# Letting each operation run where it ends first, with ScalarE as a third place for scaling probabilities

## The chip, the cores and the metric

The kernel runs on one core of a Trainium2 chip. The metric is the device time of one execution in microseconds (us); lower is better. Times are given as the median of several executions. The engines are named as the profile names them: PE is TensorE's matrix multiplication and PEld its weight load, DVE is VectorE, ACT is ScalarE, POOL is GpSimd, SP is SyncE.

## The reference

Two small transformer blocks run one after the other on one sequence of 512 tokens with 1024 features, all in float32. The first block has a layer of sparse attention (three gated branches: compressed, selected and windowed keys), a layer of windowed attention with a learned sink, and after each a feed-forward block with a short convolution. The second has a layer that mixes windowed attention with pooling over windows, a layer that mixes latent attention with a gated linear recurrence, and a squared-relu feed-forward block after each.

```python
def one_block(qb):                       # first layer, a block of 128 queries
    p_c = softmax(where(valid, sc, NEG)) * valid
    p_s = softmax(ss); p_w = softmax(where(m_w, sw, NEG))
    ...
    return gg[..., 0:1] * o_c + gg[..., 1:2] * o_s + gg[..., 2:3] * o_w
...
def conv_ffn(h, w_in, conv_w, conv_b, w_out):
    u = h @ w_in
    c = conv_b + conv_w[0] * up[:, 0:s] + ...   # three taps
    a, gate_in = split(c, 2)
    return (silu(a) * gate_in) @ w_out
...
def sq_relu_mlp(h, w1, w2):
    u = relu(h @ w1)
    return (u * u) @ w2
```

## The kernel before

Activations lie with features on the partitions and the 512 tokens along the free dimension. A float32 product is made of three products of rounded numbers: each operand is split into a high and a low part (`split` for activations, `load` for weights), and TensorE multiplies high by high, high by low and low by high (`mm3`). Every weight unit (128 x 1024) is fetched by a DMA into one of four `raw` buffers, copied to its high part, and the low part is the difference of the two (`copy` and `sub` in `load`); high and low lie in one of three `W` buffers.

The program is not written in the order in which it runs. Each helper call is recorded as an operation with an engine, its inputs and outputs, and, for some, alternatives on other engines (`alt`). A planner (`Recorder.order`) then plays the engines forward in time, with prices from `price` (cost: how long the engine is held; lat: when the result is there; lock: which other engine's use of SBUF it has to wait for). An engine that is free walks through its list of ready operations, ordered by rank (the recorded number, 1500 lower for weights), and takes the first that fits a buffer. The planned order is what is emitted; the chip then runs each engine's instructions in that order, with waits where data are needed. All instructions have one line in the profile, L698, the one that emits them.

Where an operation has an alternative, its first engine takes it whenever it comes to it. Another engine takes it when the work listed for the first engine (up to 12 ready operations, wherever they stand in the list, also those that can't start yet for want of a buffer) reaches a threshold:

```python
if op.eng != e:
    queue = sum(o.cost for _, _, o in ready[op.eng][:12] if not o.done)
    if queue + max(0, free_at[op.eng] - now) < SPILL[op.eng, e]:
        continue
```

Copies (`copy`) belong to ACT, with DVE as the other engine from 2.0 us; subtractions (`sub`, `tt(..., spare)`) belong to DVE, with POOL from 1.5 us; the scaling of a row of probabilities (`norm`) belongs to POOL, with DVE from 1.5 us; products by `ptt` are POOL's alone, and `tt` without `spare` is DVE's alone.

The stages follow one another: sparse attention (called nsa), feed-forward with convolution, windowed attention (swa), the same feed-forward again, pooling with attention (even), feed-forward (mlp), recurrence with latent attention (odd), mlp. In an attention stage the order of heads, query blocks and products is written out by hand in `ORDERS`. For a head, `scores` multiplies queries by keys, takes the maximum (DVE), the exponential with its sum (ACT), the reciprocal (DVE) and scales (`norm`); `product` transposes the probabilities on TensorE, splits them and multiplies by the values. In nsa, `norm` multiplies by the reciprocal and by the gate in one instruction with two scalars per row. ACT loads a table before a function that the loaded one doesn't hold; the planner holds such an operation back for up to `PATIENCE` (3 us) if its list still has others that need no load.

Of the kernel before, what the change touches and what calls it, by code (L numbers as in the profile page):

```python
# [11 lines left out]
AF = mybir.ActivationFunctionType  # L12
OP = mybir.AluOpType
AX = mybir.AxisListType

P = 128
S = 512
D = 1024
# [319 lines left out]
def _width(v):  # L338
# [13 lines left out]
SPILL = {("vector", "gpsimd"): 1.5, ("gpsimd", "vector"): 1.5, ("scalar", "vector"): 2.0, ("scalar", "gpsimd"): 2.0,  # L352
         ("vector", "scalar"): 1.0}
BOOST = 0
DMAQ = 2.0
HORIZON = 3000
ORDERS = {
# [28 lines left out]
PATIENCE = 3.0  # L386
# [4 lines left out]
class Recorder:  # L391
# [115 lines left out]
    def order(self):  # L507
# [4 lines left out]
        free_at = dict.fromkeys(engines, 0.0)  # L512
# [14 lines left out]
        front = 0  # L527
# [9 lines left out]
                heapq.heappush(wait[e], (op.ready, op.n, op))  # L537


        def oldest(kind):  # L540
            w = waiting[kind]
            while first[kind] < len(w) and w[first[kind]] in given:
                first[kind] += 1
            return w[first[kind]] if first[kind] < len(w) else -1
# [49 lines left out]
        while left:  # L594
# [7 lines left out]
            for e in engines:  # L602
# [6 lines left out]
                i = -1  # L609
                while i < min(len(ready[e]) - 1, 200):  # L610
                    i += 1
                    op = ready[e][i][2]
                    if op.done:
                        del ready[e][i]
                        i -= 1
                        continue
                    if op.eng != e:
                        queue = sum(o.cost for _, _, o in ready[op.eng][:12] if not o.done)
                        if queue + max(0, free_at[op.eng] - now) < SPILL[op.eng, e]:
                            continue  # L620
                    if e == "scalar" and op.table and table not in op.table and now - op.ready < PATIENCE:
                        if now - switched < PATIENCE or any(not o.table or table in o.table for _, _, o in ready[e][i + 1:]):
                            heapq.heappush(events, max(switched, op.ready) + PATIENCE + 1e-6)
                            continue
                    if e == "sync" and dma_free - now > DMAQ:
# [87 lines left out]
def F(ap):  # L713
    return ap.bitcast(F32)


def _body(tc, ctx, d, out):
# [74 lines left out]
    def tt(o, a, b, op, spare=False):  # L792
        kw = dict(out=o, in0=a, in1=b, op=op)
        nc.vector.tensor_tensor(**kw, alt=[["gpsimd", "tensor_tensor", (), kw]] if spare else None)

    def norm(o, i, a, b):
        nc.gpsimd.tensor_scalar(o, i, a, b, op0=OP.mult, op1=OP.mult, alt=[
            ["vector", "tensor_scalar", (o, i, a, b), {"op0": OP.mult, "op1": OP.mult}]])

    def ptt(o, a, b, op):  # L800
        nc.gpsimd.tensor_tensor(out=o, in0=a, in1=b, op=op)

    def sub(o, a, b):
        tt(o, a, b, OP.subtract, True)
# [168 lines left out]
    def rope(ps, cs, half):  # L973
        x, o = get(), get()
        copy(x, ps)
        if half == 32:
            for r in range(0, P, 32):
                nc.sync.dma_start(o[r:r + 32], x[r ^ 32:(r ^ 32) + 32])
            sw = o
        else:  # L980
            sw = get()
            nc.vector.stream_shuffle(sw, x, [n ^ 16 for n in range(32)])
        y = get()
        ptt(y, x, cs[0], OP.mult)
        tt(o, sw, cs[1], OP.mult)
        tt(o, o, y, OP.add, True)
        return o

# [72 lines left out]
    def nsa(x, epi, prepare, half):  # L1061
# [189 lines left out]
        def scores(g, qb, ty, h0):  # L1251
# [18 lines left out]
            for i in range(nh):  # L1270
                ei = F(e)[:, i * wd:(i + 1) * wd]
                act(ei, pv[:, i], AF.Exp, bias=nm[:, i:i + 1], accum_out=sm[:, i:i + 1])
            nc.vector.reciprocal(sm[:, 0:nh], sm[:, 0:nh])
            for i, (r, t) in enumerate(who):
                ei = F(e)[:, i * wd:(i + 1) * wd]
                gi = 3 * (4 * g + r) + t
                norm(ei, ei, sm[:, i:i + 1], gates[:, qb, gi:gi + 1])
                heads[g, qb, t, r] = ei

        def product(g, qb, ty, kb):  # L1280
# [23 lines left out]
    def sink_attn(qs, ks, vs, group, per, window, mask, sink, outs):  # L1304
# [5 lines left out]
        def scores(g, qb, h0):  # L1310
# [28 lines left out]
            nc.vector.reciprocal(sm[:, 0:per], sm[:, 0:per])  # L1339
            for i in range(per):  # L1340
                ei = ev[:, i, base:base + wd]
                norm(ei, ei, sm[:, i:i + 1], 1.0)
                heads[g, qb, h0 + i] = ei
            if over:
                nc.gpsimd.memset(ev[:, :, sc], 0.0)
# [175 lines left out]
    def odd(x, rb, half):  # L1521
# [185 lines left out]
        def scores(n, qb):  # L1707
# [7 lines left out]
            nc.vector.tensor_reduce(out=nm[:, 0:1], in_=ps, axis=AX.X, op=OP.max, negate=True)  # L1715
            act(F(e), ps, AF.Exp, bias=nm[:, 0:1], accum_out=sm[:, 0:1])
            nc.vector.reciprocal(sm[:, 0:1], sm[:, 0:1])
            norm(F(e), F(e), sm[:, 0:1], 1.0)
            es[n, qb] = e

        sums = {}
# [141 lines left out]
```

## Time and profile before

| | us |
|---|---|
| median of 3 executions | 2403.03 (2398.35 to 2403.59) |
| the profiled execution | 2399.78 |
| its span, first to last instruction | 2397.9 |
| TensorE busy in the span | 2280.3 (95%) |
| DVE busy | 1760.9 (73%) |
| POOL busy | 1254.6 (52%) |
| ACT busy | 701.8 (29%) |
| mean granted clock of TensorE | 0.976 of full speed |

The busy times are those of one execution. The share of an engine over the whole span is a mean over stages that differ much, so the rows below are taken by stage. In them a group of instructions is named by line, engine, operation and tiles (out<-in); S and D are tiles of 512 and 1024 columns in SBUF, `raw` and `W` the weight buffers, `bank` is PSUM, `small` holds 16 columns, `par` and `cst` are parameters and constants.

### The profile page before, as it was taken

What the parts mean: (1) busy time and instruction counts of PE and PEld (TensorE: products, weight loads), DVE (VectorE), ACT (ScalarE), POOL (GpSimd) and SP (SyncE); (2) the same over time, 40 slices, a digit from 0 to 9 for tenths busy, and PEclk for the clock granted to TensorE, in tenths of its full rate; (3) what the DMA queues carried; (4) which work ended last, traced back from release to release, by engine and by line L of the source; (5) the groups of instructions that cost most, each with busy time, mean ns of one, the idle gap of its engine ahead of it and who ended that gap; (6) DMA issues with size and microseconds to landing.
All of it is one profiled execution on the core that took longest, in us unless ns stands there. A gap on an engine that the chain in (4) does not pass through costs nothing.

```text
span 2397.9 us, 28536 instructions
## 1 busy us (share of the span) xinstructions
PE 2280.3 (95%) x10565; PEld 1857.6 (77%) x10565; DVE 1760.9 (73%) x2429; ACT 701.8 (29%) x1353; POOL 1254.6 (52%) x865
## 2 busy tenths in 40 slices
PE   9878999999999799999999799999999789999998
PEld 7766678888888578888888578888887568888888
DVE  7978888949499999949499897345358899643546
ACT  4435653202023463202014342000014584100003
POOL 5755636444447855444437745444466565444445
PEclk9979999999999899999999899999999989999999
DMA  6421102232225212332225213332243201222224
GB/s 208 137 75 49 54 23 88 97 106 97 97 84 185 87 36 85 101 106 97 97 82 182 71 52 99 102 109 97 97 154 115 66 27 62 97 97 97 97 97 132
DMA packets 77243, 230.02 MB, mean 96 GB/s; under 512 B 10288, under 2 KB 12976, under 8 KB 77104
## 3 DMA queue, kind: packets, MB, share of 16 engines
q1 hardware_dynamic: 75584, 226.89, 29.1%
q8 instruction: 83, 1.36, 0.2%
q10 hardware_dynamic: 1520, 1.32, 0.2%
q14 instruction: 56, 0.46, 0.1%
HBM read 206.67 MB, written 8.39 MB: 90 GB/s over the span
## 4 chain that ended last, share of the span: by engine, by line
PE 56%; DVE 6%; ACT 2%; issue 1%; POOL 1%; SPq 0%; DMA 0%; DVEq 0%; ACTq 0%; POOLq 0%
PE bank L698 56%; DVE S L698 4%; DVE small L698 1%; ACT S L698 1%; DVE D L698 1%; POOL S L698 0%; DVE W L698 0%; ACT W L698 0%; ACT L698 0%; POOL W L698 0%; ACT D L698 0%; SPq L698 0%; DVE bank L698 0%; DMA S<-S 0%; DVEq L1850 0%
## 5 line engine op out<-in xcount | busy, mean ns | idle before, releaser
L698 PE MATMUL bank<-S,W 128*128 128x512 f32 (+1 forms) x7972 | 1809.3, 387 | 9.9 <-POOL W L698 5.9
L698 PEld LDWEIGHTS bank<-S,W 128*128 128x128 f32 x7972 | 1472.6, 189 | 313.3 <-DVE S L698 7.8
L698 POOL TENSOR_TENSOR W<-raw,W 128x1024 fp32r<-128x1024 f32 (+2 forms) x288 | 693.3, 2408 | 708.3 <-DVE W L698 541.8
L698 DVE CAST W<-raw 128x1024 fp32r<-128x1024 f32 (+2 forms) x246 | 179.8, 731 | 460.5 <-issue 319.3
L698 POOL TENSOR_TENSOR S<-S,S 128x512 f32<-128x512 f32 (+3 forms) x203 | 327.4, 1618 | 234.7 <-DVE S L698 157.7
L698 ACT ACTIVATE S<-S 128x512 f32<-128x512 f32 (+2 forms) x220 | 137.4, 627 | 969.6 <-DVE S L698 951.9
L698 DVE TENSOR_TENSOR S<-bank,S 128x512 f32<-128x512 f32 (+5 forms) x429 | 264.5, 632 | 14.5 <-ACT S L698 7.0
L698 DVE SCALAR_TENSOR_TENSOR S<-S,par,S 128x511 f32<-128x511 f32 (+3 forms) x236 | 250.2, 1069 | 7.7 <-ACT S L698 2.6
L698 ACT ACTIVATE W<-raw 128x1024 fp32r<-128x1024 f32 (+2 forms) x132 | 133.7, 1015 | 298.2 <-PE bank L698 242.8
L698 DVE TENSOR_TENSOR S<-S,S 128x512 fp32r<-128x512 f32 (+3 forms) x210 | 193.4, 926 | 16.8 <-ACT S L698 4.7
L698 PE MATMUL bank<-S,D 128*128 128x512 f32 (+3 forms) x387 | 138.4, 431 | 26.1 <-DVE S L698 13.5
L698 DVE CAST S<-S 128x512 fp32r<-128x512 f32 (+1 forms) x126 | 120.2, 954 | 48.7 <-ACT S L698 44.0
L698 ACT ACTIVATE S<-bank,small 128x256 f32<-128x256 f32 (+6 forms) x245 | 127.5, 530 | 83.3 <-DVE small L698 74.8
L698 ACT ACTIVATE S<-bank 128x512 fp32r<-128x512 f32 (+5 forms) x179 | 102.8, 588 | 137.9 <-PE bank L698 116.1
L698 PE MATMUL bank<-D,W 128*128 128x512 f32 x536 | 139.8, 397 | 0.6 <-DVE W L698 0.6
L698 DVE TENSOR_TENSOR W<-raw,W 128x1024 fp32r<-128x1024 f32 (+2 forms) x90 | 124.7, 1385 | 13.6 <-ACT W L698 13.0
L698 PE MATMUL bank<-cst,S 128*128 128x128 f32 x710 | 115.5, 283 | 13.6 <-DVE S L698 7.9
L698 DVE TENSOR_REDUCE small<-bank 128x1 f32<-128x512 f32 (+7 forms) x201 | 119.9, 614 | 6.8 <-PE bank L698 5.2
L698 PEld LDWEIGHTS bank<-D,W 128*128 128x128 f32 x536 | 99.1, 188 | 20.4 <-ACT S L698 0.8
L698 PEld LDWEIGHTS bank<-cst,S 128*128 128x128 f32 x710 | 88.0, 145 | 33.8 <-DVE S L698 8.3
L698 DVE TENSOR_SCALAR S<-S,par 128x512 f32<-128x512 f32 (+1 forms) x62 | 112.3, 1812 | 2.1
L698 PEld LDWEIGHTS bank<-S,D 128*128 128x128 f32 x387 | 70.4, 197 | 51.4 <-DVE S L698 24.9
(122 smaller groups left out, 1398.3 us busy)
## 6 DMA issues: line engine op xcount, KB each, us to landing
raw<-in_f_in_dram SPq DMA_DIRECT2D x88, 512.0 KB, 3.2
raw<-in_m_out_dram SPq DMA_DIRECT2D x72, 512.0 KB, 3.2
raw<-in_m_in_dram SPq DMA_DIRECT2D x64, 512.0 KB, 3.3
raw<-in_f_out_dram SPq DMA_DIRECT2D x32, 512.0 KB, 3.2
raw<-in_a_in_dram SPq DMA_DIRECT2D x17, 512.0 KB, 3.5
raw<-in_o_in_dram SPq DMA_DIRECT2D x15, 512.0 KB, 3.4
S<-S SPq DMA_DIRECT2D x116, 64.0 KB, 2.0
raw<-in_f_out_dram SPq DMA_DIRECT2D x16, 384.0 KB, 2.9
```

Of the source, the lines that this page charges most:

```text
L698: r = getattr(getattr(nc, op.eng), name)(*args, **kw)
```

## The change

Four things change in the planner and its helpers. First, whether an engine takes an operation that has alternatives is decided by a comparison (`best`): for every engine that could do it, the planner adds the time until that engine is free and the costs of the operations of its own that stand ahead in its list (of the first 12), or the time until the other engine's hold on SBUF ends, to the operation's lat and to a tax of once its cost on POOL and DVE (none on ACT). An engine that isn't the one with the earliest end leaves the operation alone. Second, `norm` has one scalar per row and may run on ACT too; the gate of the nsa stage is multiplied into the reciprocals ahead of it, in a small product on DVE for each call of `scores`. Third, `ptt` may run on DVE and the second product of `rope` on POOL. Fourth, when the planner asks whether an ACT operation that needs a table load should be held back, operations beyond its horizon of 3000 recorded operations no longer count as others that need none.

```diff
--- before.py
+++ after.py
@@ -352,6 +352,9 @@
 SPILL = {("vector", "gpsimd"): 1.5, ("gpsimd", "vector"): 1.5, ("scalar", "vector"): 2.0, ("scalar", "gpsimd"): 2.0,
          ("vector", "scalar"): 1.0}
 BOOST = 0
+TAX = {"gpsimd": 1.0, "vector": 1.0}
+MARGIN = {}
+DEEP = 12
 DMAQ = 2.0
 HORIZON = 3000
 ORDERS = {
@@ -537,6 +540,29 @@
                 heapq.heappush(wait[e], (op.ready, op.n, op))
 
 
+        def cost_on(op, e):
+            return (op.cost, op.lat, op.lock) if e == op.eng else op.alt[e][1]
+
+        def best(op, e):
+
+            def wait(x):
+                lock = cost_on(op, x)[2]
+                return max(0.0, held["P"] - now) if lock == "D" else max(0.0, held["D"] - now) if lock else 0.0
+            here = wait(e) + cost_on(op, e)[1] + TAX.get(e, 0.0) * cost_on(op, e)[0]
+            for x in (op.eng, *op.alt):
+                if x == e:
+                    continue
+                q = max(0.0, free_at[x] - now)
+                for _, _, o in ready[x][:DEEP]:
+                    if o is op:
+                        break
+                    if not o.done and o.eng == x:
+                        q += o.cost
+                there = max(q, wait(x)) + cost_on(op, x)[1] + TAX.get(x, 0.0) * cost_on(op, x)[0]
+                if there + MARGIN.get((x, e), 0.0) < here:
+                    return False
+            return True
+
         def oldest(kind):
             w = waiting[kind]
             while first[kind] < len(w) and w[first[kind]] in given:
@@ -614,12 +640,12 @@
                         del ready[e][i]
                         i -= 1
                         continue
-                    if op.eng != e:
-                        queue = sum(o.cost for _, _, o in ready[op.eng][:12] if not o.done)
-                        if queue + max(0, free_at[op.eng] - now) < SPILL[op.eng, e]:
-                            continue
+                    if op.alt and not best(op, e):
+                        continue
                     if e == "scalar" and op.table and table not in op.table and now - op.ready < PATIENCE:
-                        if now - switched < PATIENCE or any(not o.table or table in o.table for _, _, o in ready[e][i + 1:]):
+                        if now - switched < PATIENCE or any(
+                                (not o.table or table in o.table) and o.n <= front + HORIZON
+                                for _, _, o in ready[e][i + 1:]):
                             heapq.heappush(events, max(switched, op.ready) + PATIENCE + 1e-6)
                             continue
                     if e == "sync" and dma_free - now > DMAQ:
@@ -793,12 +819,14 @@
         kw = dict(out=o, in0=a, in1=b, op=op)
         nc.vector.tensor_tensor(**kw, alt=[["gpsimd", "tensor_tensor", (), kw]] if spare else None)
 
-    def norm(o, i, a, b):
-        nc.gpsimd.tensor_scalar(o, i, a, b, op0=OP.mult, op1=OP.mult, alt=[
-            ["vector", "tensor_scalar", (o, i, a, b), {"op0": OP.mult, "op1": OP.mult}]])
+    def norm(o, i, a):
+        nc.gpsimd.tensor_scalar(o, i, a, None, op0=OP.mult, alt=[
+            ["vector", "tensor_scalar", (o, i, a, None), {"op0": OP.mult}],
+            ["scalar", "activation", (o, i, AF.Copy), {"scale": a}]])
 
     def ptt(o, a, b, op):
-        nc.gpsimd.tensor_tensor(out=o, in0=a, in1=b, op=op)
+        kw = dict(out=o, in0=a, in1=b, op=op)
+        nc.gpsimd.tensor_tensor(**kw, alt=[["vector", "tensor_tensor", (), kw]])
 
     def sub(o, a, b):
         tt(o, a, b, OP.subtract, True)
@@ -982,7 +1010,7 @@
             nc.vector.stream_shuffle(sw, x, [n ^ 16 for n in range(32)])
         y = get()
         ptt(y, x, cs[0], OP.mult)
-        tt(o, sw, cs[1], OP.mult)
+        tt(o, sw, cs[1], OP.mult, True)
         tt(o, o, y, OP.add, True)
         return o
 
@@ -1271,10 +1299,16 @@
                 ei = F(e)[:, i * wd:(i + 1) * wd]
                 act(ei, pv[:, i], AF.Exp, bias=nm[:, i:i + 1], accum_out=sm[:, i:i + 1])
             nc.vector.reciprocal(sm[:, 0:nh], sm[:, 0:nh])
+            gi = 3 * (4 * g + who[0][0]) + who[0][1]
+            if qb == 0:
+                gv = gates[:, qb, gi - 1:gi + 5].rearrange("p (r t) -> p r t", t=3)[:, :, 1:3]
+                sv = sm[:, 0:nh].rearrange("p (r t) -> p r t", t=2)
+            else:
+                gv, sv = gates[:, qb, gi:gi + 3 * nh - 2:3], sm[:, 0:nh]
+            tt(sv, sv, gv, OP.mult)
             for i, (r, t) in enumerate(who):
                 ei = F(e)[:, i * wd:(i + 1) * wd]
-                gi = 3 * (4 * g + r) + t
-                norm(ei, ei, sm[:, i:i + 1], gates[:, qb, gi:gi + 1])
+                norm(ei, ei, sm[:, i:i + 1])
                 heads[g, qb, t, r] = ei
 
         def product(g, qb, ty, kb):
@@ -1339,7 +1373,7 @@
             nc.vector.reciprocal(sm[:, 0:per], sm[:, 0:per])
             for i in range(per):
                 ei = ev[:, i, base:base + wd]
-                norm(ei, ei, sm[:, i:i + 1], 1.0)
+                norm(ei, ei, sm[:, i:i + 1])
                 heads[g, qb, h0 + i] = ei
             if over:
                 nc.gpsimd.memset(ev[:, :, sc], 0.0)
@@ -1715,7 +1749,7 @@
             nc.vector.tensor_reduce(out=nm[:, 0:1], in_=ps, axis=AX.X, op=OP.max, negate=True)
             act(F(e), ps, AF.Exp, bias=nm[:, 0:1], accum_out=sm[:, 0:1])
             nc.vector.reciprocal(sm[:, 0:1], sm[:, 0:1])
-            norm(F(e), F(e), sm[:, 0:1], 1.0)
+            norm(F(e), F(e), sm[:, 0:1])
             es[n, qb] = e
 
         sums = {}
```

## Rows read from the trace of the kernel before

**Rows 1.** Sum over the four feed-forward stretches: length, each engine's busy time.

```profile
sum 1555.00, PE 1554.26 PEld 1280.70 DVE 1033.05 ACT 263.85 POOL 748.57; mean PE 388.56 PEld 320.17 DVE 258.26 ACT 65.96 POOL 187.14
```

**Rows 2.** The four attention stages: us, engines busy (instructions), PEclk, DMA share, GB/s.

```profile
100.00:370.00 270.00, 236.56 (x1231) 182.11 (x1231) 231.25 (x440) 142.74 (x375) 149.15 (x175) 0.92 0.17 51
800.00:890.00 90.00, 72.57 (x386) 59.52 (x385) 82.36 (x183) 52.60 (x167) 56.49 (x95) 0.91 0.13 42
1290.00:1450.00 160.00, 141.57 (x676) 112.76 (x676) 145.16 (x274) 62.67 (x133) 106.98 (x83) 0.95 0.24 76
1830.00:1995.00 165.00, 134.24 (x558) 102.98 (x557) 145.73 (x201) 112.21 (x185) 100.68 (x79) 0.92 0.22 67
sum 685.00, PE 584.94 PEld 457.37 DVE 604.50 ACT 370.21 POOL 413.31; mean PE 146.23 PEld 114.34 DVE 151.12 ACT 92.55 POOL 103.33
```

**Rows 3.** TensorE's waits, whole span: us in total, times, longest us.

```profile
PE bank L698 <- DVE S L698: 33.3, 25, 6.3
...
PE bank L698 <- ACT S L698: 23.6, 12, 10.7
...
PE bank L698 <- POOL S L698: 16.3, 11, 4.6
...
PE bank L698 <- POOL D L698: 9.9, 1, 9.9
...
PE bank L698 <- ACT D L698: 8.5, 4, 4.5
...
PE bank L698 <- POOL W L698: 5.9, 4, 2.5
```

**Rows 4.** POOL's groups: count | busy us, mean ns | idle before, releaser.

```profile
L698 POOL TENSOR_TENSOR W<-raw,W 128x1024 fp32r<-128x1024 f32 (+2 forms) x288 | 693.3, 2408 | 708.3 <-DVE W L698 541.8 <-ACT W L698 70.0 <-ACT S L698 67.4
...
L698 POOL TENSOR_TENSOR S<-S,S 128x512 f32<-128x512 f32 (+3 forms) x203 | 327.4, 1618 | 234.7 <-DVE S L698 157.7 <-ACT S L698 66.8 <-issue 3.4
...
L698 POOL TENSOR_SCALAR S<-S,small,gates 128x384 f32<-128x384 f32 (+3 forms) x107 | 71.6, 679 | 60.2 <-DVE small L698 53.5 <-PE bank L698 6.1
...
L698 POOL TENSOR_SCALAR S<-S,small 128x256 f32<-128x256 f32 (+3 forms) x97 | 57.5, 602 | 45.2 <-DVE small L698 40.7 <-DVE bank L698 4.0
```

**Rows 5.** DVE's groups by shape, 400 to 650 us, a feed-forward stretch.

```profile
L698 DVE TENSOR_TENSOR W<-raw,W 128x1024 fp32r<-128x1024 f32 x14 | 17.1, 1219 | 0.0
...
L698 DVE TENSOR_TENSOR S<-S,S 128x512 f32<-128x512 f32 x16 | 11.1, 693 | 1.5
```

**Rows 6.** DVE's groups by shape in the even stage, 1290 to 1450 us.

```profile
L698 DVE TENSOR_TENSOR S<-S,S 128x512 f32<-128x512 f32 x10 | 13.3, 1347 | 0.0
...
L698 DVE TENSOR_TENSOR small<-D,cst 128x16 f32<-128x16 f32 x4 | 6.9, 1732 | 0.0
```

**Rows 7.** DVE on the small tiles: duration ns min/median/max.

```profile
L698 DVE TENSOR_SCALAR S<-S,small x25: 286/571/2486, 799.1 to 1988.3; 128x256 f32<-128x256 f32 x16, 128x384 f32<-128x384 f32 x5, 128x512 f32<-128x512 f32 x3, 128x128 f32<-128x128 f32 x1
...
L698 DVE TENSOR_TENSOR small<-small,gates x4: 178/184/208, 146.5 to 294.0; 128x16 f32<-128x16 f32 x4
```

**Rows 8.** Chain that ended last, 1930 to 1940 us: start us, us, what.

```profile
1933.59 5.72 POOL S L698 x8
```

**Rows 9.** DVE's groups, whole span.

```profile
L698 DVE CAST W<-raw 128x1024 fp32r<-128x1024 f32 (+2 forms) x246 | 179.8, 731 | 460.5 <-issue 319.3 <-PE bank L698 141.0
...
L698 DVE TENSOR_SCALAR S<-S,small 128x256 f32<-128x256 f32 (+3 forms) x25 | 21.4, 866 | 0.2
...
L698 DVE TENSOR_SCALAR S<-S,small,gates 128x256 f32<-128x256 f32 (+3 forms) x16 | 15.8, 992 | 0.1
```

**Rows 10.** Instructions on the raw weight tiles, four attention stages: sum.

```profile
sum 685.00, DVE 40.90 ACT 38.92 POOL 100.19; mean DVE 10.23 ACT 9.73 POOL 25.05
```

**Rows 11.** ACT's groups, whole span.

```profile
L698 ACT ACTIVATE W<-raw 128x1024 fp32r<-128x1024 f32 (+2 forms) x132 | 133.7, 1015 | 298.2 <-PE bank L698 242.8 <-issue 43.9 <-POOL W L698 7.3
...
L698 ACT ACTIVATE S<-bank,small 128x256 f32<-128x256 f32 (+6 forms) x245 | 127.5, 530 | 83.3 <-DVE small L698 74.8 <-issue 3.6 <-PE bank L698 3.3
...
L698 ACT ACTIVATE S<-S,small 128x512 f32<-128x512 f32 x10 | 6.9, 721 | 0.0
```

## The prediction

> **What bounds the kernel now.** Read the stretches first. Seven tenths of the span are feed-forward blocks in which TensorE is never without work: 1554.26 of 1555 us busy [rows 1]. No edit to who copies or scales what can shorten these. The rest that matters are the four attention stages, 685 us together, where TensorE is busy 584.94 us, so it idles 100.1 us, and where the granted clock is 0.91 to 0.95 [rows 2]. Length times missing clock over the four rows is 270 x 0.08 + 90 x 0.09 + 160 x 0.05 + 165 x 0.08 = 50.9 us of work lost to the lower of the two clock levels. So each idle microsecond comes with about 0.51 us lost to the clock. This pair, 151 us, is all the change can work on.
>
> Second, who TensorE waited for. Waits put down to POOL are 16.3 + 9.9 + 5.9 = 32.1 us, to ACT 23.6 + 8.5 = 32.1 us, the largest single row is DVE with 33.3 us [rows 3]. In the four stages DVE is busy 604.5 of 685 us (88%), POOL 413.3 and ACT 370.2 (54%) [rows 2]. So DVE is nearly full, POOL is slow rather than full, and ACT has room.
>
> Third, the price of an operation on each engine. A weight unit's low part takes POOL 2.408 us, a 128x512 product of two SBUF tiles about 1.618 us, and a scaling of probabilities 0.679 or 0.602 us [rows 4]. Where POOL is little in the way, DVE does the first in 1.219 and the second in 0.693 us [rows 5]. But DVE's operations on SBUF stretch while POOL works on SBUF: in the even stage ten such products take 1.347 us, not 0.693, and four tiny 128x16 products take 1.732 us, where a tiny product elsewhere takes 0.184 [rows 6, 7]. That is 10 x 0.654 + 4 x 1.548 = 12.7 us of stretch in 14 instructions.
>
> Last, a place on the chain that ended last: in the odd stage 5.72 us of it are eight instructions of POOL in a row [rows 8].
>
> **The change part by part.** The planner's prices, which stand in the code, tell only where an operation will go; what that costs I take from the trace.
>
> *Weights, high parts.* Before, DVE takes a copy as soon as 2.0 us are queued on ACT, and the copies that wait for a weight buffer count as queue; so DVE has 246 of them at 0.731 us [rows 9]. Now a queue counts only up to the operation itself. The planner prices ACT's end at 1.06 and DVE's, with the tax, at 1.30, so a copy goes to ACT unless ACT is occupied for over 0.24 us. In the feed-forward blocks this is free: TensorE is covered there by three weight buffers, and without that cover each copy would be 1.015 - 0.731 = 0.28 us later. In the four stages DVE spends 40.90 us on the raw tiles [rows 10]; if copies and subtractions are equal in number that is 40.90 / (0.731 + 1.219) = 21 of each: 21 x 0.731 = 15.4 us off DVE.
>
> *Weights, low parts.* POOL spends 100.19 us on them in the four stages [rows 10], 100.19 / 2.408 = 41.6 instructions. The planner now prices DVE at 2.37 and POOL at 4.74, so POOL gets one only behind more than 2.37 us of earlier work on DVE. On DVE they cost 1.219 us. Bounds: none moves, 0; all move, 41 x 1.219 = 50 us on DVE. DVE is 88% busy and these units rank early; I take half, 25 us.
>
> *Probabilities.* 256 scalings: 107 + 97 on POOL (71.6 + 57.5 us) [rows 4], 16 + 25 on DVE (15.8 + 21.4 us) [rows 9], and a handful in double buffers. Now the planner prices a 256-wide one at 0.42 on ACT, 0.62 on DVE, 0.92 on POOL, so most go to ACT. ACT's nearest rows are its 512-wide scaled copy at 0.721 us and its exponentials, of the same mix of widths, at 0.530 us [rows 11]. All of them on ACT would be 256 x 0.530 = 136 us: 370 + 136 + 20 (copies) = 526 of 685 us, 77%. DVE loses its 37.2 us, POOL up to 129 us.
>
> *A row against this.* DVE's fastest (narrow) scalings take 0.286 us [rows 7], less than ACT's rows, yet in place they average 0.87 to 0.99 us [rows 9]: what counts is the stretch. The Trainium skill, page ScalarE: Activation LUTs, section Rules for kernel authors, says to multiply on VectorE and not on ScalarE. By that rule the 37.2 us would stay on DVE and the sum below would lose 19 us of its gain.
>
> *The gate product.* The gate was the second scalar of the scaling; it becomes a tiny DVE product behind each of 88 reciprocals of the first stage. Nearest row: the same shape of work with the gates, 0.184 us [rows 7]. 88 x 0.184 = 16.2 us on DVE. It is added to the chain reciprocal, scaling, transpose too; many heads are in flight, so I price the delay at nothing (if it were bare, 88 x 0.184 again).
>
> *Products that gain a second engine.* Those of rotation tables, sums of squares and gates, POOL only so far, may go to DVE; one product of the rotation, DVE only so far, may go to POOL. What POOL does in the four stages besides weights and scalings is 413 - 100 - 129 = 184 us, at 1.618 us about 114 products; under half of them are of this kind (most of the others could run on either engine already), some 50. None to half may move, 0 to 25 x 0.693 = 17 us on DVE. I take 8.
>
> *Table switches.* Only far-off operations are left out of the test that delays a switch; at most 3 us at each of few switches ahead of the odd stage, on an engine with room: 0, hidden by ACT's idle time.
>
> *Sums.* DVE: -37.2 - 15.4 + 25 + 16.2 + 8 = -3.4 us. Stretch: 12.7 us are seen in one stage, so 13 us at least and 13 x 685 / 160 = 54 us at most over four; POOL's load falls from 413 to about 230 us, by near half; I take a third of the middle, 11 us. DVE in all -14.4 us. Of this I put half on the path, an estimate between a third (33.3 of 100.1 us of idle time are put down to it [rows 3]) and the 88%: -7. POOL's waits: the work behind them has an engine twice as fast, or ACT: half of 32.1 goes, -16. ACT's waits grow with its load from 54 to 77%: a quarter of 32.1, +8. Together -15 us idle, with the clock (x 0.51) another -7.5: -22.5 us. The profiled execution took 2399.8 us (span 2397.9 and 1.9 outside), 3.2 us under the median of 2403.0. So 2377 for such an execution, 2381 us for a median.
>
> **The rivals.**
>
> *DVE becomes more of a bound (slower).* Place: the four stages. All low parts and half the products move to it: -52.6 + 50 + 16.2 + 17 = +31 us, and the stretch stays because POOL keeps its other two-input work. Half on the path +15.5, ACT's +8, POOL's waits turned into waits for DVE and so not saved: 23.5 x 1.51 = +35, so 2435 us; with two thirds of the moves about 2415. It decides from the point where more than 35 of the 41 subtractions sit on DVE and still average 1.3 us or more. For it: they rank ahead of nearly everything, and DVE at 88% has 80 us free. Against it: the planner sees DVE's queue and prices POOL's hold.
>
> *ACT takes the place of POOL (same).* ACT's waits grow by 23 us instead of 8, as scalings and copies of 1.015 us stand in front of exponentials: -16 - 7 + 23 = 0, so 2400 to 2403 us. For it: in the odd stage ACT is already busy 112 of 165 us [rows 2], and 32 scalings at 0.721 us make that 135. Against it: it has 315 us free overall. To the same case counts that the change does little: the written order still sets what TensorE does next, and the new shares only move idle time.
>
> *The stretch goes altogether (much faster).* All of POOL's 32.1 us of waits and 54 / 2 of DVE's stretch, less 8 for ACT: -51, with the clock about -77; half of that gives 2361 us, 2345 is its outer end. Against it: the halo sums of the even stage and half the subtractions stay on POOL.
>
> **How the numbers follow.** Chances: forecast (2365 to 2396 us) 0.50; much faster 0.13; same 0.14; slower by DVE 0.23. Two executions of this kernel differ by 0.2% (2398.35 to 2403.59), which is about what can be told from no change. Below 2398 fall the first two: 0.63; within 2398 to 2408 0.14; above 0.23. The range leaves out the outer part of both outer cases: 2348 to 2420 us; the likeliest case alone is 2365 to 2396.
>
> **What would show it.** Right: ACT has most scalings and nearly all weight copies; POOL's waits in TensorE's list are about 16 us; DVE's mean for SBUF products in the even stage falls below 1.0 us; idle TensorE in the four stages falls from 100 to some 85 us and their clock rises. Wrong: low parts on DVE in the stages number over 35 with unchanged means; or waits for ACT pass 45 us; or the feed-forward blocks show idle TensorE, which would mean that a weight unit comes late from its new engines.

## The result, and the profile after

The changed kernel takes 2366.66 us (median of four executions, 2363.67 to 2367.2) against 2403.31 us for the kernel before in the same job: a ratio of 0.985, 95% interval 0.9833 to 0.9867. The profiled execution took 2367.2 us (before: 2399.78), with a span of 2365.3 us and a mean granted clock of 0.980 (before: 0.976).

The page's first part and the clock line over 40 slices:

```profile
PE 2274.2 (96%) x10561; PEld 1856.1 (78%) x10565; DVE 1733.0 (73%) x2825; ACT 961.1 (41%) x1649; POOL 229.1 (10%) x262
...
PEclk9979999999999999999999999999999899999999
```

POOL has lost four fifths of its work (1254.6 us before), ACT has gained 259 us, and DVE is no busier, although it executes 2825 instructions where it had 2429.

The stretches that answer to [rows 1] and [rows 2]: first the sum over four feed-forward stretches, then the four attention stages. The edges lie earlier now, and the feed-forward stretches leave out some us more at the ends of the blocks (1515 us instead of 1555), so their busy times are not compared.

```profile
sum 1515.00, PE 1513.87 PEld 1259.70 DVE 977.91 ACT 440.03 POOL 80.43; mean PE 378.47 PEld 314.92 DVE 244.48 ACT 110.01 POOL 20.11
```

```profile
95.00:365.00 270.00, 237.49 (x1211) 181.26 (x1215) 242.36 (x585) 176.31 (x440) 47.92 (x49) 0.92 0.18 54
785.00:875.00 90.00, 79.22 (x418) 63.58 (x417) 81.89 (x203) 63.88 (x192) 21.44 (x43) 0.94 0.16 51
1275.00:1420.00 145.00, 139.37 (x676) 112.34 (x675) 136.02 (x309) 80.92 (x165) 22.16 (x21) 0.98 0.27 83
1797.00:1962.00 165.00, 135.40 (x563) 103.29 (x562) 152.33 (x246) 122.82 (x200) 28.68 (x21) 0.93 0.22 67
sum 670.00, PE 591.48 PEld 460.46 DVE 612.60 ACT 443.93 POOL 120.20; mean PE 147.87 PEld 115.12 DVE 153.15 ACT 110.98 POOL 30.05
```

The feed-forward blocks still have no hole. In the stages TensorE idles 670 - 591.48 = 78.5 us where it idled 100.1: 0.9 us less in the first stage, 6.7 in the second, 12.8 in the third and 1.2 in the fourth. The even stage (third row) shows it best: the same 676 matmuls fit into 145 us where they had 160, at a clock of 0.98 instead of 0.95.

TensorE's waits, whole span, beside [rows 3]:

```profile
PE bank L724 <- DVE S L724: 30.4, 25, 4.8
PE bank L724 <- ACT S L724: 30.3, 28, 7.0
PE bank L724 <- DVE D L724: 7.4, 6, 2.6
PE bank L724 <- ACT W L724: 3.4, 5, 0.9
...
PE bank L724 <- ACT D L724: 1.5, 2, 1.1
PE bank L724 <- POOL S L724: 1.0, 2, 0.6
```

Waits for POOL's S, D and W tiles are down from 32.1 us to 1.0 (a wait of 1.5 us for a small tile of POOL stands in both lists). ACT's are 30.3 + 3.4 + 1.5 = 35.2 us, 3 more than before. DVE's largest row is 30.4 instead of 33.3.

What DVE, ACT and POOL do now (groups of the whole span), beside [rows 4], [rows 5], [rows 6], [rows 7], [rows 9] and [rows 11]. The first line is of the kernel before:

```profile
L698 DVE TENSOR_TENSOR W<-raw,W 128x1024 fp32r<-128x1024 f32 (+2 forms) x90 | 124.7, 1385 | 13.6 <-ACT W L698 13.0
...
L724 DVE TENSOR_TENSOR W<-raw,W 128x1024 fp32r<-128x1024 f32 (+2 forms) x378 | 497.9, 1318 | 76.2 <-ACT W L724 74.8
L724 DVE TENSOR_TENSOR S<-bank,S 128x512 f32<-128x512 f32 (+6 forms) x428 | 265.7, 634 | 200.5 <-PE bank L724 191.6 <-ACT S L724 5.6
L724 DVE TENSOR_TENSOR S<-S,S 128x512 f32<-128x512 f32 (+3 forms) x381 | 263.0, 698 | 14.7 <-ACT S L724 6.1 <-DMA S<-S 3.6
...
L724 DVE TENSOR_SCALAR S<-S,par 128x512 f32<-128x512 f32 (+1 forms) x109 | 57.9, 533 | 3.8
...
L724 DVE TENSOR_SCALAR S<-S,small 128x256 f32<-128x256 f32 (+3 forms) x72 | 27.1, 388 | 1.1
...
L724 DVE TENSOR_TENSOR small<-small,gates 128x1 f32<-128x1 f32 (+3 forms) x92 | 15.2, 168 | 0.6
```

```profile
L724 ACT ACTIVATE W<-raw 128x1024 fp32r<-128x1024 f32 (+3 forms) x372 | 385.7, 1037 | 959.6 <-PE bank L724 854.4 <-issue 96.0 <-DMA raw<-in_a_cmp_dram 3.5
...
L724 ACT ACTIVATE S<-S,small 128x256 f32<-128x256 f32 (+3 forms) x131 | 75.2, 593 | 25.5 <-DVE small L724 24.9
```

```profile
L724 POOL TENSOR_TENSOR S<-S 128x512 f32<-128x512 f32 x66 | 68.8, 1044 | 532.1 <-DVE S L724 523.2 <-issue 4.4 <-DMA raw<-in_m_out_dram 4.3
L724 POOL TENSOR_SCALAR S<-S,small 128x256 f32<-128x256 f32 (+3 forms) x51 | 54.1, 1064 | 199.6 <-DVE small L724 160.6 <-ACT S L724 19.6 <-PE bank L724 16.1
L724 POOL TENSOR_TENSOR S<-S,S 128x512 f32<-128x512 f32 (+3 forms) x34 | 51.7, 1532 | 225.7 <-ACT S L724 131.3 <-issue 34.3 <-DVE S L724 28.8
```

All 378 low parts of the weights sit on DVE (before: 90 there, 288 on POOL), 372 of 378 high parts on ACT. POOL has 34 operations on two S tiles instead of 203; they are called products here, although the group holds sums and differences too. The rule moved more than the prediction's parts name: POOL's largest group is now 66 squares (4 before), which ACT had done, and DVE scales 109 S tiles by a column where it scaled 62. DVE's stretch is gone over the span: its products take 698 ns on the whole span, the rate that [rows 5] showed in a feed-forward stretch, and a scaling of probabilities 388 ns (mixed widths) instead of 866 and 992. Without the weights' parts DVE was busy 1456 us before (1760.9 less 179.8 for 246 casts and 124.7 for 90 low parts) and is now busy 1231.5 us (1733.0 less 497.9 and 3.6), although that rest has 348 more instructions.

In the even stage, by shape, beside [rows 6]:

```profile
L724 DVE TENSOR_TENSOR W<-raw,W 128x1024 fp32r<-128x1024 f32 x18 | 22.8, 1268 | 0.7 <-ACT W L724 0.2
L724 DVE TENSOR_TENSOR S<-S,S 128x512 f32<-128x512 f32 x22 | 15.6, 724 | 0.6 <-DMA S<-S 0.6
...
L724 DVE TENSOR_TENSOR small<-D,cst 128x16 f32<-128x16 f32 x4 | 0.7, 164 | 0.0
```

A product there takes 724 ns instead of 1347, one of the four tiny ones 164 instead of 1732. The raw weight tiles in the four stages, beside [rows 10], and the place in the odd stage, on the chain of work, that answers to [rows 8]:

```profile
sum 670.00, DVE 76.00 ACT 58.75; mean DVE 19.00 ACT 14.69
```

```profile
1930.67 2.61 POOL S L724
```

One wait for POOL is left there, of 2.61 us instead of 5.72. Where along the span the time came from is seen on the first fetch of each stage's weights; the rows of the tensors `in_b_in`, `in_e_in` and `in_o_in` (windowed attention, even and odd stage) give the first and last issue, first for the kernel before:

```profile
L698 SPq DMA_DIRECT2D raw<-in_b_in_dram x10: 328/333/532, 729.1 to 770.3; - x10
L698 SPq DMA_DIRECT2D raw<-in_e_in_dram x11: 332/333/339, 1265.4 to 1314.2; - x11
L698 SPq DMA_DIRECT2D raw<-in_o_in_dram x19: 328/333/527, 1767.1 to 1882.1; - x19
...
L724 SPq DMA_DIRECT2D raw<-in_b_in_dram x10: 328/333/527, 721.4 to 764.4; - x10
L724 SPq DMA_DIRECT2D raw<-in_e_in_dram x11: 333/390/912, 1247.2 to 1296.6; - x11
L724 SPq DMA_DIRECT2D raw<-in_o_in_dram x19: 328/333/527, 1733.7 to 1854.3; - x19
```

So the kernel is 7.7 us ahead at the first, 18.2 at the second, 33.4 at the third, and 32.6 at the end. The odd stage, the last, gains next to nothing.

### The profile page after: what moved, and what is told of

It is laid out like the page before. It is cut to its first block, busy times and chain, and to the rows that moved or that the text cites. A ratio compares the mean times of both kernels' runs of the same rounds, so it can differ in the third digit from the quotient of the medians.

```text
span 2365.3 us, 28379 instructions
## 1 busy us (share of the span) xinstructions
PE 2274.2 (96%) x10561; PEld 1856.1 (78%) x10565; DVE 1733.0 (73%) x2825; ACT 961.1 (41%) x1649; POOL 229.1 (10%) x262
## 4 chain that ended last, share of the span: by engine, by line
PE 77%; DVE 8%; ACT 3%; issue 2%; DMA 1%; SPq 1%; POOL 0%; DVEq 0%; ACTq 0%; POOLq 0%
PE bank L724 77%; DVE S L724 5%; ACT S L724 3%; DVE small L724 1%; DVE D L724 1%; DMA S<-S 1%; DVE W L724 1%; SPq L724 1%; DMA D<-D 0%; POOL S L724 0%; ACT W L724 0%; ACT D L724 0%; ACT L724 0%; DVE bank L724 0%; DVEq L1884 0%
## 5 line engine op out<-in xcount | busy, mean ns | idle before, releaser
L724 PEld LDWEIGHTS bank<-S,W 128*128 128x128 f32 x7988 | 1477.7, 189 | 318.8 <-ACT S L724 10.5
L724 ACT ACTIVATE W<-raw 128x1024 fp32r<-128x1024 f32 (+3 forms) x372 | 385.7, 1037 | 959.6 <-PE bank L724 854.4
L724 DVE TENSOR_TENSOR W<-raw,W 128x1024 fp32r<-128x1024 f32 (+2 forms) x378 | 497.9, 1318 | 76.2 <-ACT W L724 74.8
L724 DVE TENSOR_TENSOR S<-bank,S 128x512 f32<-128x512 f32 (+6 forms) x428 | 265.7, 634 | 200.5 <-PE bank L724 191.6
L724 DVE TENSOR_TENSOR S<-S,S 128x512 f32<-128x512 f32 (+3 forms) x381 | 263.0, 698 | 14.7 <-ACT S L724 6.1
L724 ACT ACTIVATE S<-S 128x512 fp32r<-128x512 f32 (+2 forms) x220 | 137.0, 627 | 242.2 <-DVE S L724 175.8
L724 DVE SCALAR_TENSOR_TENSOR S<-S,par,S 128x511 f32<-128x511 f32 (+3 forms) x239 | 178.7, 752 | 4.1 <-ACT S L724 0.3
L724 PE MATMUL bank<-S,D 128*128 128x512 f32 (+1 forms) x356 | 135.1, 443 | 14.4 <-DVE S L724 9.4
L724 ACT ACTIVATE S<-bank 128x512 fp32r<-128x512 f32 (+4 forms) x176 | 101.5, 590 | 60.2 <-PE bank L724 51.7
L724 POOL TENSOR_TENSOR S<-S 128x512 f32<-128x512 f32 x66 | 68.8, 1044 | 532.1 <-DVE S L724 523.2
L724 PEld LDWEIGHTS bank<-S,D 128*128 128x128 f32 x356 | 66.4, 198 | 38.5 <-DVE S L724 15.2
L724 ACT ACTIVATE S<-S,small 128x256 f32<-128x256 f32 (+3 forms) x131 | 75.2, 593 | 25.5 <-DVE small L724 24.9
```

What stands on the lines that cost most here:

```text
L724: r = getattr(getattr(nc, op.eng), name)(*args, **kw)
```

## The experiments

Theory 1: the gain is POOL's two-input work (the weights' low parts) leaving POOL, so that DVE's operations no longer stretch and POOL's waits go. Theory 2: it is ScalarE as a third place for the scalings. Theory 3: it is the luck of a newly drawn plan. In the first four kernels below, and in the second of the last group, the planner's order is kept as it is, and operations are given to another engine after the planning; the others are planned anew. A range stands behind each median; ratios are to the kernel before in the same job.

**One move undone in the order of the kernel after.** All 378 low parts written out on POOL, or the 126 scalings of probabilities that ACT has (shortened: `low` and `scaling` stand for tests on the operation):

```diff
         ops = self.order()
+        for op in ops:
+            if low(op) and op.eng == "vector":          # first run
+                op.eng, op.fn = "gpsimd", options["gpsimd"]
+            if scaling(op) and op.eng == "scalar":      # second run
+                op.eng, op.fn = "gpsimd", options["gpsimd"]
```

> The order of the changed kernel is kept; after planning, the 378 weight low parts that stand on DVE are emitted on POOL. Theory 1 (the gain is POOL's two-input work leaving POOL: TensorE no longer waits for POOL and DVE no longer stretches): most of the 37 us is lost, 2390 to 2405 us, DVE's mean for 128x512 products of SBUF tiles goes from 0.70 back above 0.9 us, waits for POOL return to 15 us or more. Theory 2 (the gain is the scalings on ACT): 2365 to 2373 us. Theory 3 (the gain is a luckier plan, whichever engine has what): no forecast of its own, since the order stays; 2366 within 5.

> The order of the changed kernel is kept; after planning, the scalings of probabilities that stand on ACT (about 130) are emitted on POOL. Theory 1: POOL is 10% busy and does one-input work at 0.6 to 0.8 us, so little is lost, 2364 to 2373 us. Theory 2: half or more of the gain is lost, 2385 us or more, with waits for POOL of 15 us or more.

Measured: low parts back 2448.95 us (2441.88 to 2453.25), ratio 1.0198 [1.0173, 1.0222], 82 us above the kernel after and beyond the range of every theory; scalings back 2387.97 us (2385.16 to 2389.94), ratio 0.9942 [0.9927, 0.9957]. DVE's groups with the low parts on POOL:

```profile
L733 DVE TENSOR_TENSOR S<-S,S 128x512 f32<-128x512 f32 (+3 forms) x381 | 422.3, 1117 | 146.5 <-ACT S L733 132.7 <-DMA S<-S 5.4
...
L733 DVE TENSOR_TENSOR S<-bank,S 128x512 f32<-128x512 f32 (+6 forms) x428 | 265.5, 633 | 207.0 <-PE bank L733 186.3 <-ACT S L733 17.8
...
L733 DVE TENSOR_SCALAR S<-S,par 128x512 f32<-128x512 f32 (+1 forms) x109 | 115.2, 1058 | 3.8
```

The same 381 products take 1117 instead of 698 ns, the same 109 scalings by a column 1058 instead of 533; the 428 sums that read one operand from PSUM take 633 against 634 ns. Apart from the subtractions DVE has the same instructions in the same order, so this stretch is caused by POOL's subtractions, and the operations that suffer read SBUF alone. The Trainium skill, page SBUF — State Buffer, section Who interferes with whom, says that a DVE instruction with two SBUF inputs contends with a GpSimd instruction that reads SBUF, and that one with at most one SBUF input, outside the two-port modes, does not; these rows agree (the page counts tensor_scalar among the operations that can enter such a mode). TensorE's waits for DVE's S tiles nearly double, to 58.3 us, and it waits 11.8 us for POOL's W tiles. That bears out Theory 1 as far as its cause goes, but the 82 us, more than twice the whole gain, do not measure the gain: this order was planned for low parts on DVE.

Where the stretch lies matters too. In the four attention stages (95 to 385, 800 to 895, 1320 to 1475 and 1860 to 2045 us in this run) DVE's work without the raw tiles grows from 537 to 625 us; the rest of its growth, about four fifths, is in the feed-forward blocks, where TensorE had no hole in the kernel before. And in the even stage the subtractions are not the only cause. Its 22 products of 128x512 take 1068 ns with the subtractions back on POOL. With the subtractions off POOL but in the order of before (the next experiment), where POOL keeps its 203 products, the 10 products on DVE take 919 ns. Both lie between the 724 ns of the kernel after and the 1347 ns of the kernel before. The four tiny products, in the first and in the second of these runs:

```profile
L733 DVE TENSOR_TENSOR small<-D,cst 128x16 f32<-128x16 f32 x4 | 0.7, 163 | 0.0
...
L707 DVE TENSOR_TENSOR small<-D,cst 128x16 f32<-128x16 f32 x4 | 2.7, 685 | 0.0
```

The kernel before has 1732 there, so the subtractions by themselves do not stretch these four. The scalings' 21 us seemed to speak for Theory 2, but see the last group.

**One move alone in the order of the kernel before.** The 288 low parts that POOL had, on DVE; then also the 240 high parts that DVE had, on ACT. The edit is the same loop the other way round.

> The order of the kernel before is kept; after planning, the 288 weight low parts that stand on POOL are emitted on DVE. Theory 1: faster, 2375 to 2393 us, with DVE's stretch gone (128x512 products of SBUF tiles at 0.75 us or less) and waits for POOL at half or less of 32 us; not all of the gain, because the order was made for POOL. Theory 2: same or slower than before, 2400 to 2425 us, because a DVE that was 88% busy in the attention stages gets 50 us more. Theory 3: 2403 within 5.

> The order of the kernel before is kept; after planning, all weight low parts are emitted on DVE and all weight high parts on ACT. Low parts alone gave +6 us in this order. If DVE was then too full in the attention stages (theory 1 with its price), taking the copies off it gives that back: 2385 to 2400 us, waits for DVE below the 51 us of that run. If it is the order that doesn't suit (theory 3), 2405 us or more.

Measured: 2408.37 us (2404.26 to 2410.79), ratio 1.0024 [1.0015, 1.0033]; and 2408.28 us (2407.57 to 2411.65), ratio 1.0035 [1.0022, 1.0048]. Neither is faster than the kernel before. TensorE's waits in the first:

```profile
PE bank L707 <- DVE S L707: 43.7, 37, 8.5
...
PE bank L707 <- POOL S L707: 13.6, 11, 4.8
PE bank L707 <- POOL D L707: 12.5, 1, 12.5
...
PE bank L707 <- DVE D L707: 7.9, 9, 1.6
PE bank L707 <- DVE W L707: 6.2, 7, 2.0
```

POOL's waits for W are gone, and DVE's products fall from 926 to 787 ns over the span. But waits for DVE grow from 33.3 to 43.7 us on S tiles and from 1.2 to 6.2 us on W tiles, and POOL's S and D waits (26.1 us, [rows 3]: 26.2) stay: they do not go with the subtractions. With the high parts on ACT as well, DVE's S waits are 39.9 us. So Theory 1 in its simple form, which expected 2375 to 2393 us, fell: in the new order the low parts have to be off POOL, and in the old order that is not enough. That an order planned for low parts on POOL puts them where DVE is wanted fits both runs and was not tried further.

**Rule and helpers apart, each planned anew.** The rule alone (`best` with the helpers of before), and the helpers alone (gates' product, `norm` with a place on ACT, `ptt` and the rotation's product with a second engine) under the old thresholds. The test on table switches is the old one in the first and the new one in the second. Shortened:

```diff
 # rule alone: the helpers as before
-                    if op.eng != e:
-                        queue = sum(o.cost for _, _, o in ready[op.eng][:12] if not o.done)
-                        ...
+                    if op.alt and not best(op, e):
+                        continue
 # helpers alone: the old test, with a threshold for the new place
-         ("vector", "scalar"): 1.0}
+         ("vector", "scalar"): 1.0, ("gpsimd", "scalar"): 1.5}
```

> The planner's comparison of ends in the kernel before, planned anew; the scalings keep two scalars and POOL or DVE, the products of POOL alone and of DVE alone stay so, the switch test is the old one. Theory 1 (POOL's two-input work has to leave, with the weights' copies going to ACT in the same plan): most of the gain, 2368 to 2385 us, POOL under 25% busy. Theory 2 (scalings on ACT are what pays, and the first run of scalings put back on POOL gave 21 us of 37): 2385 to 2400 us, waits for POOL of 12 us or more. Both allow 10 us either way for a newly drawn plan.

> The old rule (another engine helps from 1.5 us of queue on) with the new helpers: scalings may go to ACT, products of POOL to DVE, the second rotation product to POOL, the gate in a product of its own; planned anew. Theory 1: little, 2393 to 2412 us, because the weights' low parts stay on POOL and DVE's operations stay stretched (its casts of SBUF tiles near 0.95 us). Theory 2: half the gain or more, 2385 us or less.

Measured: rule alone 2383.42 us (2382.48 to 2384.06), ratio 0.9928 [0.9913, 0.9943]; helpers alone 2446.98 us (2446.95 to 2447.32), ratio 1.0193 [1.0176, 1.021]. The rule alone puts all low parts on DVE too and gives about half the gain. The helpers alone lie outside both expectations; the last group says why. What the rule alone leaves on POOL are 135 products of two S tiles (34 in the kernel after), and all of TensorE's waits for POOL's S tiles are in the first stage:

```profile
L722 POOL TENSOR_TENSOR S<-S,S 128x512 f32<-128x512 f32 (+3 forms) x135 | 207.8, 1547 | 986.2 <-ACT S L722 574.3 <-DVE S L722 402.3 <-PE bank L722 4.3
```

```profile
PE bank L722 <- ACT S L722: 34.2, 26, 13.8
PE bank L722 <- DVE S L722: 31.0, 27, 4.8
PE bank L722 <- POOL S L722: 15.8, 5, 8.9
```

**How much a new draw of the plan moves.** Two edits that mean nothing by themselves: `TAX` of the kernel after from 1.0 to 1.02, and the two 1.5 us thresholds between DVE and POOL of the kernel before to 1.52.

> The changed kernel with the tax on DVE and POOL at 1.02 instead of 1.0: a change that means nothing but makes the planner draw another plan. Theories 1 and 2: 2366 within 6 us, POOL as idle as before this edit. Theory 3: it moves by 10 us or more either way.

> The kernel before with its two thresholds of 1.5 us between DVE and POOL at 1.52: means nothing, draws another plan. The changed kernel moved by 10 us under such an edit. Theories 1 and 2: 2403 within 12 us. Theory 3 (the gain is in the draw): it may come out as low as 2375.

Measured: 2357.07 us (2351.66 to 2361.74), ratio 0.9814 [0.9795, 0.9832], which is 9.6 us below the kernel after (8.7 by the ratios); and 2404.49 us (2403.37 to 2404.93), ratio 1.0015 [1.0006, 1.0024]. So one of two such edits moved a planned kernel by nearly 10 us, with the busy times of DVE, ACT and POOL within 5 us of what they were. That is more than Theories 1 and 2 allowed for and less than Theory 3 asked for. Neither draw comes near the 37 us of the change, so two draws do not bear out Theory 3 alone; but a difference of 10 us between two plans is no evidence of anything else.

**The scalar that was dropped.** In the second run POOL's scalings were far slower than in the kernel before; the change had taken away their second scalar (the gate, or 1.0). The next kernels multiply by 1.0 again on POOL, each in the order of its counterpart with one scalar:

```diff
-        nc.gpsimd.tensor_scalar(o, i, a, None, op0=OP.mult, alt=[
+        nc.gpsimd.tensor_scalar(o, i, a, 1.0, op0=OP.mult, op1=OP.mult, alt=[
```

That edit alone; with the scalings back on POOL; with the helpers alone; and, as a candidate, with `TAX` at 1.02:

> The kernel after in its own order; each of the 57 scalings that GpSimd keeps multiplies by the divisor and by 1.0 (two scalars, as before the change) where the change left one. In the kernel after a 128x512 one takes 1670 ns on GpSimd, in the kernel before 753 to 802 ns with two scalars. If the count of scalars makes that difference, GpSimd's 57 scalings fall from a mean of some 1.3 us to some 0.65 and its busy time by 30 to 40 us; its waits in the kernel after are some 2.5 us, so the time falls by 0 to 4 us, to 2362 to 2367. If the difference is one of the place (other work beside it), GpSimd's durations stay.

> The kernel after in its own order, the 126 scalings of ScalarE written out on GpSimd again, all of GpSimd's with two scalars. Theory 2 (ScalarE as a third place pays by itself): still slower than the kernel after, 2376 to 2390. If the 21 us of the run with one scalar came from the doubled price of the one-scalar form: 2364 to 2372, TensorE's waits for GpSimd's scalings near 3 us where they were 14.7.

> The old rule with the helpers of the change (the gates' product, the scaling with a place on ScalarE, the products with a place on VectorE), GpSimd's 193 scalings with two scalars. With one scalar this took 2446.98 us. If the doubled scalings made the harm: 187 of them at a mean of 1168 ns become some 600, GpSimd loses some 105 us of work, its waits fall from 59 us to some 30, and the time to 2395 to 2420. If the harm is that of the plan under the old rule, it stays above 2435.

> Candidate: the kernel after with the factor TAX at 1.02 in place of 1.0 (2357.07 us alone) and two scalars in GpSimd's scalings. If the two add up, 2353 to 2357 us, below both kernels.

Measured: 2366.63 us (2363.47 to 2370.13), ratio 0.9853 [0.9838, 0.9867]; 2367.97 us (2366.89 to 2370.27), 0.9861 [0.9845, 0.9878]; 2409.77 us (2408.77 to 2412.91), 1.0032 [1.0019, 1.0045]; 2353.72 us (2351.46 to 2356.05), 0.9799 [0.9784, 0.9813]. POOL's scalings by shape, with the scalings back on POOL, first with one scalar, then with two:

```profile
L733 POOL TENSOR_SCALAR S<-S,small 128x512 f32<-128x512 f32 x42 | 72.1, 1721 | 96.1 <-DVE small L733 78.5 <-ACT D L733 10.5 <-ACT S L733 3.7
...
L733 POOL TENSOR_SCALAR S<-S,small 128x256 f32<-128x256 f32 x63 | 66.2, 1058 | 78.5 <-DVE small L733 66.5 <-PE bank L733 7.8 <-DVE bank L733 2.8
```

```profile
L733 POOL TENSOR_SCALAR S<-S,small 128x256 f32<-128x256 f32 x63 | 40.3, 648 | 95.2 <-DVE small L733 76.5 <-PE bank L733 10.6 <-ACT S L733 3.1
L733 POOL TENSOR_SCALAR S<-S,small 128x512 f32<-128x512 f32 x42 | 34.6, 827 | 112.9 <-DVE small L733 86.3 <-ACT S L733 11.7 <-ACT D L733 11.6
```

With one more multiplication the same instruction on the same tile takes 48% (512 columns) or 61% (256 columns) of the time. In the kernel after it is hidden: 28 us less of POOL's work (201.1 against 229.1 us), no change of the time. With it, ACT as a third place is worth 2367.97 - 2366.63 = 1.3 us in this order, inside what can be told apart: Theory 2 falls, and 20 of its 21 us were the price of the slow form. A plan drawn without ACT as a place for scalings, all else as in the kernel after, was not tried. The slow form also made most of the harm of the helpers alone: 2446.98 becomes 2409.77 us in the same order, with waits for POOL's S tiles of 31.8 instead of 59.0 us; that is still 0.3% above the kernel before. The candidate is the fastest kernel measured, 13 us below the kernel after. The other draw alone took 2357.07 us, and the intervals overlap, so what the second scalar adds to it can't be told.

## Why the prediction was right, and where its terms were off

**The forecast** was 2381 us, within 2348 to 2420; 2366.66 came, at the faster edge of the likeliest case (2365 to 2396). Its place was right in the main: of the 26.5 us of idle time that went over the span (117.6 before, 91.1 after), 21.6 are in the four stages, and the feed-forward blocks were untouched. The sum had 15 us of idle time and 7.5 of clock; measured are the 26.5 us and 6.1 us (TensorE's busy time 2280.3 against 2274.2). So the clock gave back less for each microsecond of idle time than the factor of 1.51 said, 1.23. By the lists of waits POOL gave 31.1 us, DVE took 0.6 and ACT 3.1, together 27.4 us, beside -16, -7 and +8 in the sum. The mechanism was the one foretold, work leaving POOL; that the total stayed in the range owes something to luck, since the terms were off by 15, 8 and 5 us and not all in one direction.

**POOL's waits** were the mis-sized term: "half of 32.1 goes, -16"; 31 went. The half followed from the step on the low parts, where bounds of 0 and all were seen and half was taken, with the reason that DVE was 88% busy. All of them moved. And the runs on the old order show that even this reading was too simple: without the subtractions POOL's S and D waits stay at 26 us. In the kernel after, the products of two S tiles have gone from POOL as well: the prediction moved at most 25 in the stages, and there the group went from 71 to 13 (over the span from 203 to 34). The run of the rule alone, with 135 of them left, has 15.8 us of POOL's S waits. That it is these products which make the wait was read from this row and not tried by themselves.

**DVE's waits**: -7 forecast, +0.6 measured (before 33.3 + 8.1 + 1.2 = 42.6 us, after 30.4 + 7.4 + 2.9 + 2.5 = 43.2). DVE's work in the stages was to fall by 14.4 us and rose by 8.1 (604.50 to 612.60). The raw tiles added 35.1 us (76.00 instead of the 40.90 of [rows 10]) where the sum had 25 - 15.4 = +9.6: the half of the low parts again. Everything else fell by 27.0 us where the sum had -37.2 + 16.2 + 8 - 11 = -24, though made up otherwise: 220 more instructions, each shorter. DVE has 53 more products there than before, some 38 us of work where the sum had 8, so the relief of the stretch, taken as 11 us, was larger than that (its upper bound, 13 x 685 / 160, is 56 and not 54, which changes nothing). The run with the low parts back on POOL gives a size: the same 2441 other instructions of DVE take 1231.5 us in the kernel after and 1684.1 us there, 453 us more, of which some 80 us are in the stages. That is the price in the new order, not the relief against the kernel before.

**ACT's waits**: +8 forecast, +3 measured. ACT took 126 of the 256 scalings, about half and not most, and its load in the stages rose to 443.93 of 670 us, 66% instead of 77%. Per scaling DVE was the cheaper place once its stretch was gone (388 against 593 ns, mixed widths). The gates' product was right: 16 us for 88 forecast, 15.2 us in the row above for 92, of which 4 were there before. Its delay can't be seen in the waits.

**What was not counted**: the start. The feed-forward stretches are 1555 of 2397.9 us, 65% and not seven tenths; the 158 us that are in neither kind of stretch are the start, the end and edges. The first 100 us, before and after:

```profile
0.00:100.00 100.00, 93.18 (x418) 72.53 (x419) 86.30 (x93) 43.73 (x70) 59.67 (x53) 0.99 0.61 194
...
0.00:100.00 100.00, 97.69 (x459) 78.08 (x460) 81.56 (x129) 49.38 (x76) 16.29 (x29) 1.00 0.63 202
```

TensorE idles 2.3 us there instead of 6.8; a single wait of 4.5 us for a D tile of ACT is gone. With the 0.9 us of idle time that the first stage lost, this is most of the 7.7 us by which the weights of windowed attention are early; the second and third stage gave the next 10.5 and 15.2 us.

**The rivals.** DVE as the bound: its deciding point (over 35 of 41 subtractions on DVE, still at 1.3 us or more) was met in number and not in price. In the four stages, where it was set, all 61 low parts are on DVE at 1.22 to 1.27 us (1.318 over the whole span, 1.385 for the 90 of before). DVE's other work lost its stretch too, which the rival had denied. The kernels in the order of before, with the low parts on DVE and the products still on POOL, are this rival in small: waits for DVE's S tiles up by 10 us, time +0.2%. The rival in which the stretch goes altogether (2345 to 2361 us) was right on the stretch and on POOL's waits; its time needed DVE's waits to fall with the stretch, and they did not. Against it stood "the halo sums of the even stage and half the subtractions stay on POOL"; the halo sums stayed (10 operations, 13.6 us), no subtraction did. ACT in POOL's place did not come about (waits for ACT 35.2 us, 3 more and not 23).

**Open**: what the test on table switches does by itself was not tried; the odd stage has 18 table loads where it had 19, the whole span 29 where it had 28. How much of the 17 us between the rule alone and the kernel after is the products' second engine, how much is ACT as a place that the planner reckons with, and how much a draw of the plan, is open as well: no run gave back the products alone.

## What to carry to other kernels

When two engines slow each other, count work by what it does to the other engine's instructions: here 378 subtractions cost their own time on one engine, and 453 us on the other if they are left. Then ask where these fall: about four fifths fell in blocks where TensorE had no hole before. A change in the assignment and the order in which it runs go together; test an assignment in both orders before giving it the credit. Where a planner draws the order, change a price by 2% first and see how far the time moves: a difference of that size can't be credited to an edit.

## What the runs showed of the hardware

That a second scalar makes a scaling on POOL faster, 827 instead of 1721 ns on 128x512, in the same order of instructions with the same work beside it, was not expected. The other widths agree (384 columns: 1336 and 655 ns; 128: 669 and 407). The 20 us between the two kernels with the scalings back on POOL come from that edit alone; what in POOL makes it was not looked into.
